# Weighted sums of gathered expert rows: on TensorE by accumulating transposes of rows that ScalarE has scaled, for more of the rows than before

## The chip, the cores and the metric

The kernel runs on one core of one Trainium2 chip. The metric is the device time of one execution in microseconds (us); the median of three runs of the kernel before is 3475.92 us, the lowest 3460.99 us, the highest 3478.14 us. A core has TensorE (PE, with its weight loads shown apart as PEld), VectorE (DVE), ScalarE (ACT), GpSimd (POOL), SyncE (SP), which starts most loads, and 16 DMA engines that all queues share.

## The reference

Three blocks of a network run one behind the other on 512 tokens of 1024 features in float32: a first block (two feed-forwards around a mixer of a gated recurrence and a 31-tap convolution), a second block (a mixer with a gated delta rule, then a layer of experts), and a third block (a mixer of retention and a state space, then a feed-forward). What the change touches is the layer of experts at the end of the second block:

```
ids, gates = peer_routing(h2, ...)          # per token 8 heads x 16 experts = 128 experts
# per token: a[s] = gelu(u[id_s] . h2) * gate_s     for s = 0..127
#            ff   = sum over s of a[s] * v[id_s]    v: rows of 1024 numbers
x = x + gt2 * ff
return rms_norm(x, final_norm_w)
```

So each token needs 128 rows of a table u and 128 rows of a table v, each of 4 KB, gathered by number. The 512 tokens need 512 gathers of u and 512 of v, a gather being one row for each of 128 tokens, 512 KB.

## The kernel before, in words

The tokens lie in four tiles of 128 (tokens on the partitions), and the tiles in two halves of two tiles. The halves run one behind the other: the experts of half 0 run beside the first two blocks of half 1, and those of half 1 beside the third block of half 0 (`experts`, line 1761). Ahead of that stretch lie the first two blocks of half 0, behind it the third block of half 1.

Each engine takes its instructions in the order in which the program wrote them. The program writes the other half's phases and puts steps of the experts in between: `tick` (line 130) adds to a credit at a pace that the table `ZONE` sets for each phase, and takes the next step of the experts from the list `self.fill` whenever the credit allows. A step is one gathered tile of u or v. In the steady part the steps alternate: u of head h+1, v of head h (`order`, line 1210). The names of the phases in `ZONE` are x and g (opening, products of the first mixer), h (gated recurrence), c (convolution), f (feed-forward of the first block), m (products of the second mixer), d (delta rule), R (routing, and products of the third mixer), r (retention), s (state space), F3 (feed-forward of the third block and what is left of the experts).

A step i first starts gathers (`fetch`, line 1162, from GpSimd's queue) until 8 beyond i are under way, then works on its own. The gathered tiles, and five long-lived ones (the two h2, the running sum `acc`, and two of `finish`), share 15 buffers named `gu`; a gather waits until a buffer is free. `u_step` (line 1168) is one VectorE instruction over 128x1024 that multiplies by h2 and sums along the row into one column of `act`; after 16 of them ScalarE applies gelu and VectorE the gate.

`v_step` (line 1177) adds a[s] times a v tile to the sum, on one of two engines. The second number of `ZONE` is the share that TensorE takes: it adds up in `vcredit`, and when this reaches 1 the step goes to TensorE. There ScalarE makes a diagonal matrix dg (128x128, the identity scaled by the column a[s], two buffers), and TensorE multiplies dg with the v tile, as two products of 512 columns that accumulate in two PSUM banks over the whole tile of tokens. Every other step is one VectorE instruction, acc = v * a[s] + acc, over 128x1024. Step 127 of a tile always goes to TensorE. `finish` (line 1196) adds the two sums, applies the modulation, adds to x and normalises.

Other names: `bcast_row` (line 696) spreads a column over rows by four transposes a bank and a copy by ScalarE; `psum` (line 163) takes one of 8 PSUM banks; `put_mix` (line 829) transposes with four instructions a call.

Of the kernel before, what the change touches and what calls it, by code (L numbers as in the profile page):

```python
# [11 lines left out]
F32 = mybir.dt.float32  # L12
# [9 lines left out]
NT = 4          # token tiles  # L22
NH = 2          # token tiles of a half: the halves run one behind the other
# [11 lines left out]
# Costs of steps, in the unit of tick and idle: a transfer of 512 KB, a step of the routing, the end of a token tile  # L35
DMA, ROUTE, FINISH = 1.46, 0.8, 6.0
AHEAD = 8           # gathers under way ahead of their use
GB = 15             # their buffers
# the hidden blocks of the feed-forwards that run piece by piece in the gaps of the other half
ASIDE1 = (4, 4, 4, 4, 4, 2)  # L40
ASIDE3 = (4,) * 4
FIRST3 = 16          # hidden blocks of the third feed-forward of half 0 beside the last experts
ADA = 28             # tiles of the modulation beside the first feed-forward, the others beside the second
CONV_PE = (0, 2)     # blocks of the long convolution on TensorE, by half
# by phase: pace of the steps of the experts, share of their sums that TensorE takes
ZONE = dict(x=(1, 0.5), g=(1, 0.35), h=(1.15, 0.41), c=(0.43, 0.4), f=(1.43, 0), m=(1.73, 0.06), d=(1.09, 0.4),
            R=(1.09, 0.39), r=(1.33, 0.3), F3=(1.1, 0), s=(1, 0.65))
# pieces let in by gap of TensorE
GAP = dict(_0=4, l=3, h=0.74, c=0.22, m=5.53, d=0.9, r=0.5, s=1.6, _4=5.2, ln=8, l4=8)
NORM = 4.82          # pace of a normalisation  # L50
WEIGHTS = 3          # of a tile of weights in float32
# rates of the steps: modulation beside the two feed-forwards, experts during the routing
RATE_ADA, RATE_ROUTE = (0.85, 0.6), (0.92, 2.17)
# the course of the phases beside the experts, the transfers of their own, and the share of the experts' steps to fit in
# [3 lines left out]
class Ker:  # L58
    def __init__(self, ctx, tc, I):
# [3 lines left out]
        self.exact = False      # products in float32 itself, not in parts  # L63
# [14 lines left out]
        self.aux = nc.gpsimd        # for what VectorE need not do, unless GpSimd has transfers to start  # L78
# [3 lines left out]
        # states: of the first and of the second block, then both of the third block's retention  # L82
# [13 lines left out]
    def xt(self, es, side=None):  # L96
        """transposed activations, split in two, for one phase"""
        xp = es.enter_context(self.tc.tile_pool(name="xt", bufs=1, side=side))
        self.XH, self.XL = self.pair(xp, "X", KD)

    def pair(self, pool, name, n, **k):
        """an operand of products, n blocks: in two parts, or whole"""
        if self.exact:
            return pool.tile([P, n, TH], F32, name=name + "H", **k), None
        return [pool.tile([P, n, TH], F32R, name=name + c, **k) for c in "HL"]
# [19 lines left out]
    def course(self, i):  # L125
        """the rate that spreads the steps of the experts over a phase"""
# [3 lines left out]
    def tick(self, d, load=0.0):  # L130
        """a phase goes on by d, with load for a transfer of its own: the steps of the other half's experts
        go in between so that the transfers are even"""
# [12 lines left out]
    def idle(self, d):  # L145
        """TensorE has little to do for d: pieces of the feed-forward set aside go in between"""
# [29 lines left out]
    def rsqrt(self, out, in_, scale, eps):  # L176
        """out = (in_ * scale + eps) ** -0.5: Newton's iteration from the halved exponent"""
# [43 lines left out]
    def ahead(self):  # L221
        """of the weights of a feed-forward set aside, split the next tile and load on"""
# [9 lines left out]
    def whole(gen):  # L232
        """all pieces of a generator at once; its value"""
# [12 lines left out]
    def g_fm(self, srcs):  # L246
        """feature-major blocks: out[f, i, t] = sum_k w_i[k, f] X[t, k]; srcs [128, 8*128]"""
# [16 lines left out]
    def g_tm(self, srcs, lhs, evac):  # L264
        """token-major: out[t, c] = sum_k lhs[k, t] w[k, c]; srcs: list of [128, 2, 512]; lhs(k) -> (H, L) [128, 512]"""
# [23 lines left out]
    def stats(self, y):  # L289
        """mean and variance over the free axis (1024 or 512)"""  # L290
# [12 lines left out]
    def g_transpose_x(self, src, scale=None, bias=None):  # L303
        """XH, XL <- split of (src^T * scale + bias); src(t, k) -> [128 t, 128 feat]"""
# [18 lines left out]
    def layer_norm(self, gname, bname, alpha):  # L323
        """x <- alpha * LN(x); XT <- split of LN(x)^T"""
# [35 lines left out]
    def g_ffn(self, parts, up, down, scale, fb=0):  # L360
        """x += scale * ffn; up(pool, j): generator of blocks j and j + 1 of the hidden layer, [128, 2, TH];
        down(k, c): weights of blocks k and k + 1"""
# [164 lines left out]
    def _hgrn(self, hp, uT, acc):  # L527
# [5 lines left out]
        # lower bound: softmax over the two rows, first row  # L533
# [128 lines left out]
    def ada_setup(self):  # L662
        """modulation vectors, feature-major: mod[:, 8*i + k] = feature 128*k + p of the i-th of six"""
# [24 lines left out]
    def wide(self, pool, name, key, n=D, at=0):  # L688
        """a row on all partitions; where transfers hold the time, from its columns on TensorE"""
# [6 lines left out]
    def bcast_row(self, out, colsv):  # L696
        """out[*, 128*k + p] = colsv[p, k]"""
# [18 lines left out]
    def g_rms_xt(self, xn, scale, bias):  # L716
        """xn[t] <- x * rstd; XT <- split of (xn^T * scale + bias)"""
# [29 lines left out]
    def softplus(self, pool, z, n):  # L747
        """z <- log(1 + exp(z)), accurate for any z"""
# [17 lines left out]
    def gemm_narrow(self, pool, src, n, meta=None):  # L766
        """token-major X @ w[:, :n] -> psum [128, (t, n)]; src [128, 8*n]; with the meta tokens from 256 on"""
# [22 lines left out]
    def _mixer2(self, mp):  # L790
# [5 lines left out]
        # q, k, v: short convolution and silu, feature-major  # L796
# [1157 lines left out]
```

## Time and profile before

| what | value |
|---|---|
| median of three runs | 3475.92 us (3460.99 to 3478.14) |
| span of the profiled execution, first to last instruction | 3464.7 us |
| the profiled execution's own time | not recorded apart from its span, which lies 3.7 us over the lowest run and 11.2 us under the median |
| PE, PEld busy share of the span | 87%, 68% |
| DVE, ACT, POOL busy share | 77%, 33%, 42% |
| mean granted TensorE clock | 0.932 of full speed |
| gathers' queue | 536.94 MB |
| all other loads | 417.29 MB |

The gathers begin at about 960 us and the last expert sum ends at about 2880 us. Busy shares are over the whole span; the rows further down give them by stretch. PE's ends are modelled, and a float32 product of 512 columns stands in the trace as two records, a transpose as one.

### The profile page before, as it was taken

The numbers are of one execution on the slowest core, as the hardware profiler recorded it, in microseconds if no ns is written. First come the engines' busy times: TensorE is split into PE (matmuls) and PEld (weight loads), VectorE is DVE, ScalarE is ACT, GpSimd is POOL, SyncE is SP. The second block draws the span as 40 slices with busy tenths as digits, with TensorE's granted clock in tenths as the row PEclk, the third lists the DMA queues.
The fourth block names the chain that finished last, engine by engine and source line by source line (L and its number), as shares of the span: only waits on it lengthen the run. The fifth ranks groups of instructions, "written<-read, shape, count | busy, mean of one in ns | idle before, by whom it ended". The sixth has DMA issues, their size and how long they took to land. (4 is left out here: it accounts for less than half of the span.)

```text
span 3464.7 us, 44842 instructions
## 1 busy us (share of the span) xinstructions
PE 3023.7 (87%) x15402; PEld 2350.9 (68%) x15402; DVE 2667.9 (77%) x6456; ACT 1145.3 (33%) x1687; POOL 1439.0 (42%) x1187
## 2 busy tenths in 40 slices
PE   9999999998979789987777867879797975999998
PEld 9987889888866357836354643536474745888897
DVE  7779686665588999878898999897877786566555
ACT  4454544553312242103222121112222213455554
POOL 0020000023245656655677567586767671211200
PEclk9999999999999899998899988899998987999999
DMA  8863477542389979998999899999999995644365
GB/s 312 279 194 118 131 267 233 168 161 86 105 303 357 355 263 384 409 402 325 381 326 375 335 339 391 347 368 357 333 365 359 396 409 193 182 133 139 119 188 162
DMA packets 276757, 957.10 MB, mean 276 GB/s; under 512 B 38304, under 2 KB 42144, under 8 KB 276528
## 3 DMA queue, kind: packets, MB, share of 16 engines
q0 software_dynamic: 147456, 536.94, 41.0%
q1 hardware_dynamic: 129072, 417.29, 35.6%
q8 instruction: 122, 2.00, 0.2%
q14 instruction: 107, 0.88, 0.1%
HBM read 947.81 MB, written 2.10 MB: 274 GB/s over the span
## 5 line engine op out<-in xcount | busy, mean ns | idle before, releaser
L1164 POOL DMA_INDIRECT gu<-in_peer_v,idx x512 | 633.6, 1238 | 317.1 <-issue 111.9
L1164 POOL DMA_INDIRECT gu<-in_peer_u,idx x512 | 609.3, 1190 | 349.6 <-issue 110.9
L1171 DVE SCALAR_TENSOR_TENSOR gu<-gu 128x1024 f32<-128x1024 f32 x512 | 620.7, 1218 | 59.4 <-DMA gu<-in_peer_u,idx 55.7
L203 DVE TENSOR_TENSOR wL<-wr,wH 128x1024 fp32r<-128x1024 f32 x332 | 409.1, 1234 | 249.2 <-ACT wH L202 231.9
L256 PE MATMUL ps<-XH,wr 128*128 128x256 f32 x2368 | 528.7, 383 | 0.2 <-issue 0.2
L256 PEld LDWEIGHTS ps<-XH,wr 128*128 128x128 f32 x2368 | 450.9, 192 | 73.2 <-issue 12.8
L202 ACT CAST wH<-wr 128x1024 fp32r<-128x1024 f32 x332 | 348.3, 1050 | 440.3 <-PE ps L281 217.4
L1194 DVE SCALAR_TENSOR_TENSOR gu<-gu,act 128x1024 f32<-128x1024 f32 x366 | 467.6, 1278 | 28.6 <-DMA gu<-in_peer_v,idx 23.4
L1188 PE MATMUL ps<-gu,dg 128*128 128x512 f32 x568 | 306.5, 664 | 101.8 <-DMA gu<-in_peer_v,idx 67.4
L1188 PEld LDWEIGHTS ps<-gu,dg 128*128 128x128 f32 x568 | 112.7, 212 | 206.9 <-issue 158.2
L278 PE MATMUL ps<-wr,XH 128*128 128x512 f32 x512 | 229.1, 601 | 0.0
L256 PE MATMUL ps<-XH,wH 128*128 128x256 f32 x1408 | 206.5, 289 | 16.3 <-ACT XH L116 10.0
L256 PE MATMUL ps<-XH,wL 128*128 128x256 f32 x1408 | 202.4, 287 | 1.5 <-DVE wL L203 1.2
L256 PE MATMUL ps<-XL,wH 128*128 128x256 f32 x1408 | 203.0, 288 | 0.2
L256 PEld LDWEIGHTS ps<-XH,wH 128*128 128x128 f32 x1408 | 186.6, 196 | 21.9 <-ACT XH L116 13.7
L256 PEld LDWEIGHTS ps<-XH,wL 128*128 128x128 f32 x1408 | 185.6, 196 | 2.9 <-DVE wL L203 2.7
L203 DVE TENSOR_TENSOR fL<-fr,fH 128x1024 fp32r<-128x1024 f32 x98 | 126.1, 1288 | 79.5 <-ACT fH L202 50.1
L256 PEld LDWEIGHTS ps<-XL,wH 128*128 128x128 f32 x1408 | 186.5, 197 | 0.6 <-DVE XL L118 0.6
L278 PEld LDWEIGHTS ps<-wr,XH 128*128 128x128 f32 x512 | 98.0, 193 | 122.7 <-issue 120.3
L202 ACT CAST fH<-fr 128x1024 fp32r<-128x1024 f32 x98 | 102.6, 1047 | 175.4 <-PE ps L256 58.7
L1186 ACT ACTIVATE dg<-ident,act 128x128 f32<-128x128 f32 x142 | 55.1, 400 | 312.3 <-PE ps L1188 246.5
L184 POOL TENSOR_TENSOR r<-rx,mhalf 128x1 f32<-128x1 f32 x18 | 11.9, 669 | 330.7 <-DVE rx L182 330.7
(618 smaller groups left out, 5462.4 us busy)
## 6 DMA issues: line engine op xcount, KB each, us to landing
wr<-in_wi_fm SPq DMA_DIRECT2D x112, 512.0 KB
wr<-in_wi_tm SPq DMA_DIRECT2D x96, 512.0 KB
wr<-in_wf SPq DMA_DIRECT2D x96, 512.0 KB
wr<-in_wo SPq DMA_DIRECT2D x64, 512.0 KB
wa<-in_wada SPq DMA_DIRECT2D x48, 512.0 KB
wr<-in_f2g SPq DMA_DIRECT2D x44, 512.0 KB
wr<-in_f2u SPq DMA_DIRECT2D x44, 512.0 KB
wr<-in_f2d SPq DMA_DIRECT2D x44, 512.0 KB
```

The source lines that it names most:

```text
L184: nc.gpsimd.tensor_tensor(out=out, in0=x, in1=self.mhalf[:p, :].to_broadcast(list(out.shape)), op=ALU.pow)
L202: self.nc.scalar.copy(H, raw)
L203: self.nc.vector.tensor_tensor(out=L, in0=raw, in1=H, op=ALU.subtract)
L256: nc.tensor.matmul(ps[:, i * TH:(i + 1) * TH], a[:, k * P:(k + 1) * P], b[:, k, :], start=n == 0, stop=n == KD * len(terms) - 1)
L278: nc.tensor.matmul(pss[t], lh[:, ts], wh, start=k == 0, stop=k == nk - 1)
L1164: nc.gpsimd.indirect_dma_start(out=g, out_offset=None, in_=I[src], in_offset=bass.IndirectOffsetOnAxis(ap=idx[:, s:s + 1], axis=0))
L1171: nc.vector.scalar_tensor_tensor(g, g, 1.0, h2, op0=ALU.mult, op1=ALU.mult, accum_out=st["act"][:, s:s + 1])
L1186: nc.scalar.activation(dg, self.ident, AF.Copy, scale=c)
L1188: nc.tensor.matmul(st["ps"][i], dg, g[:, i * 512:(i + 1) * 512], start="pe" not in st, stop=s == 127)
L1194: nc.vector.scalar_tensor_tensor(st["acc"], g, c, st["acc"], op0=ALU.mult, op1=ALU.add)
```

## The change

Of the sums over v, those for TensorE are done in another way. ScalarE multiplies the gathered v tile itself, in place, by the column a[s] (128x1024 instead of the 128x128 diagonal). TensorE then adds the scaled tile to the sum by eight transposes of 128x128, which accumulate in the same two PSUM banks, so that the banks hold the sum transposed. These eight are written into the program only at the tile's next v step (`add_up`), except for step 127, whose own follow at once. `finish` copies the two banks to SBUF by ScalarE, transposes them back by eight transposes into two new banks, and goes on as before; the buffer that it copies into is filled with the row of the final norm afterwards, not before.

The second number of most entries of `ZONE`, TensorE's share, is raised: by a little under twice for most. The paces, `COURSE` and everything else stay. The diff also drops the comments, which is left out here.

```diff
-ZONE = dict(x=(1, 0.5), g=(1, 0.35), h=(1.15, 0.41), c=(0.43, 0.4), f=(1.43, 0), m=(1.73, 0.06), d=(1.09, 0.4),
-            R=(1.09, 0.39), r=(1.33, 0.3), F3=(1.1, 0), s=(1, 0.65))
+ZONE = dict(x=(1, 0.9), g=(1, 0.65), h=(1.15, 0.75), c=(0.43, 0.75), f=(1.43, 0), m=(1.73, 0.2), d=(1.09, 0.75),
+            R=(1.09, 0.7), r=(1.33, 0.6), F3=(1.1, 0.1), s=(1, 1))
...
+        def add_up(last=False):
+
+            g, st["wait"] = st["wait"], None
+            for i in range(2):
+                for j in range(4):
+                    k = 4 * i + j
+                    nc.tensor.matmul(st["ps"][i][:, j * P:(j + 1) * P], g[:, k * P:(k + 1) * P], self.ident,
+                                     is_transpose=True, start="pe" not in st and j == 0, stop=last and j == 3)
+            st["pe"] = True
+
         def v_step(s, g):
...
             c = st["act"][:, s:s + 1]
             self.vcredit += self.vshare
+            if st.get("wait") is not None:
+                add_up()
             if (self.vcredit >= 1.0 and s) or s == 127:
                 self.vcredit -= 1.0
-                dg = pp.tile([P, P], F32, name="dg", bufs=2)
-                nc.scalar.activation(dg, self.ident, AF.Copy, scale=c)
-                for i in range(2):
-                    nc.tensor.matmul(st["ps"][i], dg, g[:, i * 512:(i + 1) * 512],
-                                     start="pe" not in st, stop=s == 127)
-                st["pe"] = True
+                nc.scalar.activation(g, g, AF.Copy, scale=c)
+                st["wait"] = g
+                if s == 127:
+                    add_up(True)
...
             fw = pp.tile([P, D], F32, name="gu", bufs=GB)
-            self.bcast_row(fw, self.fw2)
+            for i in range(2):
+                nc.scalar.copy(fw[:, i * 512:(i + 1) * 512], st["ps"][i])
             for i in range(2):
                 c = slice(i * 512, (i + 1) * 512)
-                nc.vector.tensor_tensor(out=acc[:, c], in0=st["ps"][i], in1=acc[:, c], op=ALU.add)
+                pt = self.psum()
+                for j in range(4):
+                    nc.tensor.transpose(pt[:, j * P:(j + 1) * P], fw[:, (4 * i + j) * P:(4 * i + j + 1) * P], self.ident)
+                nc.vector.tensor_tensor(out=acc[:, c], in0=pt, in1=acc[:, c], op=ALU.add)
                 nc.vector.tensor_tensor(out=acc[:, c], in0=acc[:, c], in1=g2[:, c], op=ALU.mult)
                 nc.vector.tensor_tensor(out=y[:, c], in0=y[:, c], in1=acc[:, c], op=ALU.add)
+            self.bcast_row(fw, self.fw2)
```

## Rows read from the trace of the kernel before

**Rows 1.** The page's engines: busy us, share of the span, instructions.
```profile
PE 3023.7 (87%) x15402; PEld 2350.9 (68%) x15402; DVE 2667.9 (77%) x6456; ACT 1145.3 (33%) x1687; POOL 1439.0 (42%) x1187
```
**Rows 2.** Busy time by stretch, whole expert stretch: PE, PEld, DVE, ACT, POOL, clock, DMA.
```profile
955.00:2890.00 1935.00, 1587.64 (x6132) 1051.49 (x6130) 1678.63 (x4972) 416.81 (x766) 1242.88 (x1024) 0.90 0.94 355
```
**Rows 3.** The same, six stretches: phases h, d, routing, r, r, s.
```profile
1140.00:1240.00 100.00, 70.83 (x272) 41.17 (x272) 93.49 (x261) 23.91 (x44) 66.37 (x59) 0.86 0.90 324
...
1700.00:1840.00 140.00, 101.39 (x537) 71.77 (x536) 130.57 (x258) 34.55 (x61) 101.19 (x85) 0.87 0.92 328
...
1880.00:2040.00 160.00, 115.04 (x465) 80.62 (x464) 150.31 (x656) 38.53 (x72) 95.18 (x82) 0.86 0.91 343
...
2120.00:2200.00 80.00, 50.31 (x158) 28.05 (x157) 70.98 (x271) 11.66 (x21) 52.16 (x47) 0.79 0.95 355
...
2280.00:2360.00 80.00, 55.62 (x177) 30.54 (x176) 73.38 (x248) 13.77 (x24) 63.98 (x53) 0.85 0.98 375
...
2440.00:2520.00 80.00, 60.71 (x195) 33.11 (x194) 70.39 (x159) 22.95 (x49) 60.63 (x50) 0.89 0.90 332
```
**Rows 4.** The same: the first feed-forward, then two stretches of products in R.
```profile
1280.00:1540.00 260.00, 247.50 (x939) 178.51 (x938) 220.41 (x725) 36.99 (x53) 158.96 (x129) 0.97 1.01 395
...
2040.00:2120.00 80.00, 79.42 (x289) 46.25 (x288) 71.44 (x256) 15.66 (x30) 56.60 (x47) 1.00 1.01 377
...
2360.00:2440.00 80.00, 80.00 (x387) 58.05 (x386) 60.49 (x146) 20.56 (x42) 51.59 (x41) 0.98 0.96 356
```
**Rows 5.** Stretches, line 1188 alone: PE, PEld, clock, DMA; first and last of six.
```profile
1140.00:1240.00 100.00, 32.40 (x62) 11.52 (x62) 0.86 0.90 324
...
2440.00:2520.00 80.00, 28.77 (x57) 11.31 (x58) 0.89 0.90 332
```
**Rows 6.** Groups by line: engine, operation, count; busy us, mean ns; idle before.
```profile
L1194 DVE SCALAR_TENSOR_TENSOR gu<-gu,act 128x1024 f32<-128x1024 f32 x366 | 467.6, 1278 | 28.6 <-DMA gu<-in_peer_v,idx 23.4 <-issue 2.0 <-DVE rt L1303 0.7
L1188 PE MATMUL ps<-gu,dg 128*128 128x512 f32 x568 | 306.5, 664 | 101.8 <-DMA gu<-in_peer_v,idx 67.4 <-ACT dg L1186 23.6 <-issue 10.1
L1186 ACT ACTIVATE dg<-ident,act 128x128 f32<-128x128 f32 x142 | 55.1, 400 | 312.3 <-PE ps L1188 246.5 <-issue 37.7 <-DVE act L1175 14.7
L722 ACT ACTIVATE xn<-xres,r 128x1024 f32<-128x1024 f32 x12 | 13.3, 1141 | 11.0 <-DVE r L188 4.3 <-DVE rt L191 3.0 <-DVE r L192 2.8
```
**Rows 7.** Timeline of PE: start us, us, line, count of equal instructions.
```profile
1905.18 1.88 PE L1188 MATMUL ps<-gu,dg 128*128 128x512 f32 x4
...
1039.98 1.07 PE L702 MATMUL ps<-ident,grc 128*128 128x128 f32 x8 [2.13 <-DVE rt L1235]
1040.87 1.88 PE L702 MATMUL ps<-ident,brc 128*128 128x128 f32 x8
1042.55 2.78 PE L310 MATMUL ps<-ident,xres 128*128 128x128 f32 x16
```
**Rows 8.** Busy time by stretch around those transposes; the clock stands third from last.
```profile
1037.50:1040.80 3.30, 1.17 (x9) 0.85 (x9) 3.30 (x18) 0.52 (x2) 0.71 (x1) 1.00 0.30 37
1040.90:1044.30 3.40, 3.40 (x19) 3.40 (x18) 3.40 (x17) 2.68 (x6) 2.79 (x3) 0.50 0.87 310
1044.40:1047.00 2.60, 1.41 (x14) 1.21 (x13) 2.60 (x10) 2.60 (x7) 2.05 (x2) 1.00 0.89 265
```
**Rows 9.** Waits in 955 to 2890: us in total, times, longest us.
```profile
ACT dg L1186 <- PE ps L1188: 246.5, 75, 13.0
...
PE ps L1188 <- DMA gu<-in_peer_v,idx: 67.4, 12, 16.1
...
DVE gu L1171 <- DMA gu<-in_peer_u,idx: 55.7, 46, 16.5
...
POOL gu L1164 <- PE ps L1188: 31.6, 21, 4.4
```
**Rows 10.** Timeline at the end of the last tile's sums.
```profile
2863.87 15.79 DVE L1194 SCALAR_TENSOR_TENSOR gu<-gu,act 128x1024 f32<-128x1024 f32 x12
2872.79 3.75 PE L1188 MATMUL ps<-gu,dg 128*128 128x512 f32 x4 [16.12 <-DMA gu<-in_peer_v,idx]
```

## The prediction

> **What bounds the kernel now.** I read the page's engines first [rows 1]: PE 87%, DVE 77%. That is an average over three parts. The experts' gathers lie between 955 and 2890 us, so all that the change touches is in 1935 of 3464.7 us [rows 2]; ahead of it and behind it nothing is edited. In that part DVE is busy 1678.63 us (87%), the DMA engines 0.94 of the time, PE 1587.64 us, ACT only 416.81 us (22%). Three resources are close to full, so I went to single stretches. Two kinds show. In six stretches, where small products, evictions and vector work follow one another (gated recurrence, delta rule, routing, retention, state space), DVE is at 88 to 94% and PE at 63 to 76% with a clock of 0.79 to 0.89 [rows 3]. They are 640 us long together, DVE is busy 589.1 us of them (92%), DMA is at 0.92 on average (weighted by length). There VectorE is what the stretch waits for. In the stretches of large products PE is busy 79.42 and 80.00 of 80 us at clock 0.98 to 1.00, and DVE has room [rows 4]; TensorE sets their length. In the feed-forward of the first block DMA stands at 1.01 and 395 GB/s [rows 4]: I take 1.01 for what "full" looks like here. The waits agree: VectorE waits for landings of u only 55.7 us in 46 places [rows 9], so rows mostly lie ready before VectorE gets to them.
>
> **How many sums move.** Working the credits of `tick` through the program's order gives where the 512 v steps fall: x 4, g 13, h 36, c 3, f 73, m 48, d 45, R 163, r 26, s 41, F3 60. Times the shares this is 141.4 before and 261.4 after; with the forced step 127 of each tile and the carry of `vcredit` it is 142 and 262. The trace has 142 diagonals on ScalarE and 568 records of products [rows 6], four for each step. So 120 sums leave VectorE: R 52, d 15, h 13, s 13, m 9, r 7, F3 6, g 4, x 1.
>
> **VectorE.** 120 x 1278 ns [rows 6] = 153 us less.
>
> **TensorE.** Four records of a step take 1.88 us, the last one's own length is 0.59 us at full clock, so they start 0.43 us apart: a step holds TensorE 4 x 0.43 = 1.72 us [rows 7]. A transpose is one record. Eight took 1.07 us with a last one of 0.28 us, so (1.07 - 0.28) / 7 = 0.11 us apart [rows 7]: a step of eight holds it 0.9 us. Before 142 x 1.72 = 244 us, after 262 x 0.9 = 236 us: TensorE's work stays about the same though it has nearly twice the sums. No row shows a transpose that accumulates. From below it costs 0.11 us as these do; from above, were it worked as a float32 product, two records of 0.11, 0.22 us, and 461 us in all. I take 0.11: adding in PSUM costs the products nothing either, as they start as regularly.
>
> A row that bears on the clock: at 1040.9 us the granted clock fell to 0.50 (1.2 GHz), after a stretch in which PE was busy 1.17 of 3.30 us, and in the 3.40 us that followed PE ran transposes alone; behind them the clock was 1.00 again [rows 8], and the eight that began there took 1.88 us, the eight ahead of them 1.07 us [rows 7]. The Trainium skill, page "TensorE: Matmul & The Clock Gate", section "Part 4: PE-mode transpose", says that transposes do not count as activity for the clock gate, so that the full clock isn't granted for them, and that one took about 275 ns in a kernel. By its figure the sums would hold TensorE an estimated 262 x 8 x 0.275 = 576 us, 332 us more than now. Here the trace disagrees: the clock rose on transposes alone. I keep the rule as a rival.
>
> **ScalarE.** A diagonal costs 0.40 us, and the same form as the new instruction, 128x1024 with a scale by column, 1.141 us [rows 6]. 142 x 0.40 = 57 us become 262 x 1.141 = 299 us: +242 us, which takes ScalarE from 22% to 34% of the part. It lies beside other work unless a phase's eviction stands right behind it in ScalarE's queue. The new instruction waits for the gather's landing, which the diagonal did not; queued behind it are copies out of PSUM that TensorE and VectorE wait for. On the other hand ScalarE no longer waits for TensorE to release one of two diagonals, 246.5 us in 75 places now, and TensorE no longer waits for a landing itself (67.4 us in 12 places [rows 9]): it comes to the eight transposes one v step later. What is late next is VectorE's u step, at the same place in the order. Bounds: nothing gained from the waits, to 134 us of added ScalarE time in the six stretches (below) all in the chain. I take 4 us lost, near the low end, as ScalarE is busy only 15 to 29% there [rows 3].
>
> **Buffers.** A tile on TensorE is now held for one v step more. GpSimd's gathers waited for those products 31.6 us in 21 places [rows 9]; with 262 / 142 as many it would be 58 us, +27. Bounds 0 and 27; I take 2, since a gather that starts late costs only where the rows aren't ready in advance.
>
> **finish.** Each of the four adds two copies by ScalarE (0.6 us, half of a 1.14 us one), eight transposes (0.9 us) and hand-overs, some 3 us. At the end of the last tile VectorE ends its twelve sums at 2863.87 + 15.79 = 2879.66 us, TensorE its own at 2876.54 [rows 10]: 3.1 us of cover for the new steps, and the other three have gathers running ahead. I take 0; without cover 4 x 3 = 12 us.
>
> **The sum.** In the six stretches TensorE has 62, 67, 72, 26, 32 and 57 records (the first and last in [rows 5]), 316 / 4 = 79 steps; at 262 / 142 it will be 146, 67 more. VectorE loses 67 x 1.278 = 86 us of 589 and would be at 79%. These stretches could shrink by as much, but their bytes must still come: at 0.92 of the time now, against 1.01 when full, DMA leaves 640 x (1 - 0.92 / 1.01) = 57 us. So 0 to 57 us; I take 38, two thirds of it, because VectorE is the fuller one but the round trips from engine to engine remain. In four stretches of products in R (two of them in [rows 4]; 139 records) 35 x 1.72 = 60 us of TensorE become 64 x 0.9 = 58: 2 us. The other 120 - 67 - 29 = 24 sums, 31 us of VectorE, lie in the opening, m and F3, mostly beside full DMA: 0 to 31, I take 8. Together 38 + 2 + 8 - 4 - 2 = 42 us. The profiled span of 3464.7 us would become 3423; what lies around it stays, and as that span is 11.2 us under the median of the runs, the median becomes 3475.9 - 42 = 3434 us.
>
> **Rivals.**
> *All of it turns into time.* VectorE is the only bound of the six stretches and DMA gets fuller than 1.01 of any stretch: 57 + 2 + 31 = 90 us, 3386 us. For it: 92% busy. Against it: 395 GB/s in the fullest stretch, 324 to 375 in the six [rows 3, 4].
> *Hidden anyway.* The six stretches are held by the chain through TensorE, and by DMA at 0.94 on average [rows 2], so that a lighter VectorE only waits more: within 17 us, some 3470 us. For it: three resources near full. Against it: few waits of VectorE for landings.
> *ScalarE's queue, slower.* In the six stretches ScalarE gets 146 x 1.141 - 79 x 0.40 = 135 us more. Where a scaling stands right before a copy that TensorE waits for, its 1.14 us is added to the round trip, while VectorE's 1.28 us leaves it. It decides once more than 86 of the 135 us, 64%, lie in that chain; with all of them it is 135 - 86 = 49 us slower, 3525 us. For it: PE, ACT and DVE take turns in these phases, and ScalarE now stops at landings. Against it: ScalarE is idle over 70% of the time.
> *The clock, slower.* If transposes don't hold the clock, it stays at 0.50 in the six stretches, whose mean is 0.86 and in which PE is busy 453.9 us: 453.9 x 0.86 / 0.50 = 781 us in 640, 141 us slower, 3617 us. Against it: [rows 8]. That is what the page's rule would do here.
>
> **How the numbers follow.** Forecast (18 to 75 us gained) 0.50, all of it (over 75) 0.14, hidden 0.20, ScalarE's queue 0.12, clock 0.04. 0.5%, 17 us, is what a measurement of this kernel can tell; so faster 0.64, same 0.20, slower 0.16. The likeliest case alone spans 3401 to 3458. The range for 8 in 10 goes down to 3382, just past the case in which all turns into time, and up to 3486, which takes in the hidden case and a third of the price of ScalarE's queue.
>
> **What would show it.** 262 scalings of 128x1024 on ScalarE at about 1.14 us; 2096 transposes 0.11 us apart at full clock; 250 sums left on VectorE; VectorE near 80% and DMA up to 0.97 or more in phases h, d, routing and s; stretches of products unchanged in length; the part from the first gather to the last sum some 40 us shorter. Wrong would be: transposes 0.2 us apart, a lower granted clock than 0.90 over the part, long waits of TensorE for ScalarE's scaling, or GpSimd waiting for transposes far over 58 us.

## The result and the profile after

The changed kernel takes 3490.86 us (median of 5 runs), the kernel before beside it 3465.52 us: a ratio of 1.0063, 95% interval 1.0044 to 1.0082, so 22 us slower. I had forecast 3434 us, 42 us faster, from the median of the first three runs, 3475.92 us; that of the five beside the changed kernel is 10 us lower. A second measurement beside other kernels gave 1.0043 (1.0030 to 1.0056). The times differ a little from one chip to the next, so below only ratios are compared, each to runs of the kernel before on the same chip.

What the change does came out as counted. The engines of the page after, then its groups by line (columns as in [rows 6], which they answer to; the scaling is L1197, the transposes L1183, VectorE's v sums L1204):

```profile
PE 3030.0 (87%) x16962; PEld 2508.2 (72%) x16962; DVE 2541.6 (73%) x6336; ACT 1366.5 (39%) x1806; POOL 1406.1 (40%) x1187
```
```profile
L1204 DVE SCALAR_TENSOR_TENSOR gu<-gu,act 128x1024 f32<-128x1024 f32 x246 | 315.1, 1281 | 48.1 <-DMA gu<-in_peer_v,idx 43.6 <-issue 2.9
L1183 PE MATMUL ps<-ident,gu 128*128 128x128 f32 x2096 | 315.0, 300 | 143.0 <-ACT gu L1197 136.9 <-issue 5.9
L1197 ACT ACTIVATE gu<-gu,act 128x1024 f32<-128x1024 f32 x262 | 296.0, 1147 | 399.2 <-DMA gu<-in_peer_v,idx 332.5 <-DVE gu L1204 12.2 <-issue 11.3
```

262 scalings at 1.147 us, 2096 transposes, 246 sums left on VectorE (366 before; four more are the plain products that open each tile). VectorE's v sums take 315.1 us in place of 467.6, as counted; by the engines' row VectorE is busy 126 us less than in [rows 1] and TensorE 6 us more. And yet the time grew. The waits of the same part as in [rows 9] (us in total, times, longest us):

```profile
ACT gu L1197 <- DMA gu<-in_peer_v,idx: 332.5, 73, 40.3
...
PE ps L1183 <- ACT gu L1197: 136.9, 40, 22.9
DVE gu L1171 <- DMA gu<-in_peer_u,idx: 85.8, 86, 3.0
...
POOL gu L1164 <- PE ps L1183: 37.9, 18, 24.0
...
POOL gu L1164 <- ACT gu L1197: 27.8, 23, 7.4
```

ScalarE used to wait for TensorE to give back a diagonal; now it waits for landings, in 73 places. TensorE's waits for landings (67.4 us) have become waits for the scaling behind the landing, and grew to 136.9: one of the signs of being wrong that the prediction had named. ScalarE's idle time ahead of these instructions grew less, from 312.3 us ahead of diagonals [rows 6] to 399.2.

Where the time went I read by pairing equal products: the n-th TensorE instruction of a line (the sums left out) is the same work in both traces, and the difference of its start is how late the kernel is there. Before against after: 2 us late at 1010, 14 at 1090, 36 at 1321, where the feed-forward of phase f begins, 28 in phase d, 37 in the routing, 17 at 2352, 26 at the end. So nearly all is lost between 1040 and 1321 us, in x, g, h and c, where the prediction had put a gain in sum, and phase d, one of the heaviest in sums, gives nothing back.

Phases h, d, routing, r, r and s of [rows 3], bounded by the same products in the trace after (columns: stretch, length, busy us of PE, PEld, DVE, ACT, POOL, clock, DMA share, GB/s):

```profile
955.00:2920.00 1965.00, 1597.04 (x7689) 1210.59 (x7688) 1547.59 (x4855) 637.90 (x887) 1210.05 (x1026) 0.89 0.93 349
1152.00:1265.00 113.00, 71.79 (x423) 57.57 (x423) 96.41 (x395) 42.62 (x53) 66.51 (x61) 0.83 0.80 277
1722.00:1868.00 146.00, 104.95 (x734) 96.51 (x734) 115.45 (x244) 62.40 (x81) 96.17 (x84) 0.85 0.90 316
1906.00:2074.00 168.00, 119.98 (x655) 106.30 (x654) 137.48 (x621) 66.50 (x89) 96.44 (x85) 0.83 0.91 345
2154.00:2227.00 73.00, 51.75 (x233) 37.64 (x231) 68.17 (x337) 24.68 (x29) 53.38 (x44) 0.79 0.96 357
2307.00:2377.00 70.00, 55.44 (x258) 38.12 (x257) 50.66 (x108) 24.66 (x28) 48.85 (x45) 0.88 1.02 399
2460.00:2545.00 85.00, 62.94 (x329) 47.55 (x328) 65.30 (x155) 42.16 (x59) 59.76 (x51) 0.78 0.91 328
```

VectorE fell from 93 to 79% in d and from 94 to 82% in the routing, as forecast, but those stretches are 146 us against 140 and 168 against 160. DMA did not rise there (0.90 and 0.91; 0.97 or more was the sign). Only the two of phase r are shorter (73 and 70 against 80), and in the second DMA is full (1.02).

The place with TensorE's largest single wait in the opening, in phase h: ScalarE's timeline after, then TensorE's (start us, us, line, count, idle before and what ended it).

```profile
1139.23 1.15 ACT L1197 ACTIVATE gu<-gu,act 128x1024 f32<-128x1024 f32 x1 [2.64 <-DVE acc L500]
1140.28 1.05 ACT L584 COPY qT<-ps 128x512 f32<-128x512 f32 x2
1155.73 1.15 ACT L1197 ACTIVATE gu<-gu,act 128x1024 f32<-128x1024 f32 x1 [14.39 <-DMA gu<-in_peer_v,idx]
1161.04 1.15 ACT L1197 ACTIVATE gu<-gu,act 128x1024 f32<-128x1024 f32 x1 [4.16 <-DMA gu<-in_peer_v,idx]
1162.10 0.56 ACT L563 COPY vv<-ps 128x512 f32<-128x512 f32 x1
...
1168.75 0.23 ACT L1309 ACTIVATE gate<-gate 128x32 f32<-128x32 f32 x1 [4.79 <-DVE gate L1308]
...
1169.35 0.59 ACT L598 COPY kT<-ps 128x512 f32<-128x512 f32 x1
```
```profile
1147.18 1.04 PE L1183 MATMUL ps<-ident,gu 128*128 128x128 f32 x8
1148.06 0.60 PE L596 MATMUL ps<-ident,kk 128*128 128x128 f32 x4
1148.49 1.04 PE L1183 MATMUL ps<-ident,gu 128*128 128x128 f32 x8
1170.00 2.08 PE L604 MATMUL ps<-qT,kT 128*128 128x128 f32 x8 [20.47 <-ACT kT L598]
```

kT's copy out of PSUM needs the four transposes of L596, done by 1149. It runs 20 us later. Some 13 of these are two scalings ahead of it in ScalarE's queue that wait for their rows; most of the other 7 are a gate of the routing, also ahead of it, that waits for VectorE. Before, this copy was late too, by 12 us, behind an activation of 16 results of u steps:

```profile
1121.11 1.28 ACT L1174 ACT_TABLE_LOAD   x1
1146.19 0.22 ACT L1174 ACTIVATE act<-act 128x16 f32<-128x16 f32 x1 [23.80 <-DVE gu L1171]
1146.31 0.39 ACT L1186 ACTIVATE dg<-ident,act 128x128 f32<-128x128 f32 x1
1146.60 1.05 ACT L563 COPY vv<-ps 128x512 f32<-128x512 f32 x2
1147.55 0.60 ACT L598 COPY kT<-ps 128x512 f32<-128x512 f32 x1
```

One correction to what stands ahead of the prediction: the order on an engine is not that of the program's text. The framework that builds the kernel sorts each engine's instructions. With fewer v sums on VectorE it put other work there earlier: in the list of VectorE's instructions 361 of the routing and 63 sums of the short convolution stand ahead of phase h's second token tile, against 298 and 14 before, and the traces show the same shift. So each change of a share also changes the order, here and in every experiment.

### The profile page after: what moved, and what is told of

It is laid out like the page before. It is cut to its first block, busy times and chain, and to the rows that moved or that the text cites. A ratio compares the mean times of both kernels' runs of the same rounds, so it can differ in the third digit from the quotient of the medians.

```text
span 3490.5 us, 47918 instructions
## 1 busy us (share of the span) xinstructions
PE 3030.0 (87%) x16962; PEld 2508.2 (72%) x16962; DVE 2541.6 (73%) x6336; ACT 1366.5 (39%) x1806; POOL 1406.1 (40%) x1187
## 4 chain that ended last, share of the span: by engine, by line
PE 27%; DVE 9%; DMA 7%; issue 3%; ACT 2%; POOL 2%; another core or an unknown queue 0%; SPq 0%; DVEq 0%; ACTq 0%; POOLq 0%
PE ps L256 9%; DMA gu<-in_peer_v,idx 4%; DVE gu L1171 3%; PE ps L278 3%; PE ps L1183 3%; DMA gu<-in_peer_u,idx 3%; PE ps L280 2%; PE ps L281 2%; PE ps L282 2%; POOL gu L1164 1%; PE ps L1399 1%; DVE rt L1318 1%; ACT gu L1197 1%; DVE gu L1204 1%; PE ps L785 1%
## 5 line engine op out<-in xcount | busy, mean ns | idle before, releaser
L1164 POOL DMA_INDIRECT gu<-in_peer_u,idx x512 | 618.5, 1208 | 375.3 <-issue 123.5
L1164 POOL DMA_INDIRECT gu<-in_peer_v,idx x512 | 590.4, 1153 | 355.2 <-issue 130.4
L256 PE MATMUL ps<-XH,wr 128*128 128x256 f32 x2368 | 536.7, 386 | 0.0
L1197 ACT ACTIVATE gu<-gu,act 128x1024 f32<-128x1024 f32 x262 | 296.0, 1147 | 399.2 <-DMA gu<-in_peer_v,idx 332.5
L1183 PE MATMUL ps<-ident,gu 128*128 128x128 f32 x2096 | 315.0, 300 | 143.0 <-ACT gu L1197 136.9
L1183 PEld LDWEIGHTS ps<-ident,gu 128*128 128x128 f32 x2096 | 274.0, 157 | 200.0 <-ACT gu L1197 156.7
L1204 DVE SCALAR_TENSOR_TENSOR gu<-gu,act 128x1024 f32<-128x1024 f32 x246 | 315.1, 1281 | 48.1 <-DMA gu<-in_peer_v,idx 43.6
```

The source lines that it names most:

```text
L256: nc.tensor.matmul(ps[:, i * TH:(i + 1) * TH], a[:, k * P:(k + 1) * P], b[:, k, :], start=n == 0, stop=n == KD * len(terms) - 1)
L1164: nc.gpsimd.indirect_dma_start(out=g, out_offset=None, in_=I[src], in_offset=bass.IndirectOffsetOnAxis(ap=idx[:, s:s + 1], axis=0))
L1183: nc.tensor.matmul(st["ps"][i][:, j * P:(j + 1) * P], g[:, k * P:(k + 1) * P], self.ident, is_transpose=True, start="pe" not in st and j = ...
L1197: nc.scalar.activation(g, g, AF.Copy, scale=c)
L1204: nc.vector.scalar_tensor_tensor(st["acc"], g, c, st["acc"], op0=ALU.mult, op1=ALU.add)
```

## The experiments

The theories: 1, ScalarE's queue: scalings wait for landings with copies that TensorE needs behind them (1a: in phases x and g, ahead of phase h's first copies). 2, the larger shares themselves, by whatever method. 3 and 6, tiles held longer, so that gathers start late. 4, VectorE's order. 5, the clock. All ratios are to the kernel before.

**e1_method.** The table `ZONE` of before in the changed kernel, so the method alone.

> The new way of taking a sum (scaling on ScalarE, eight accumulating transposes), with the shares of before: 142 scalings, no sum more on TensorE. Theory 1 (ScalarE's queue: the scaling waits for a gather's landing, and copies out of PSUM that TensorE needs stand behind it; in the changed kernel ScalarE waits 332.5 us for landings in 73 places, and 36 us are lost between 1040 and 1321 us): with 142 / 262 of the scalings and nothing taken from VectorE a loss against before of 10 to 25 us, lost between 1040 and 1321 us again. Rival 2 (the shares: more sums on TensorE in the opening phases are what loses, however they are done): the time of before within 8 us. Rival 3 (buffers: a tile is held for one v step more, gathers start late): a loss of 10 to 25 us too, but with GpSimd waiting for transposes or scalings and not ScalarE for landings ahead of the copies that come late.

1.0056 (1.0042 to 1.0070): the method alone costs 19 us with 142 sums. That is theory 1's size. Of its place a part shows: TensorE's products start 8 us late at the beginning of f, and the rest is lost here and there behind it. Nearly all of these 8 us arise near 1045 us, where the first mixer's products begin. ScalarE and TensorE in e1, then in c_before:

```profile
1048.69 1.15 ACT L1197 ACTIVATE gu<-gu,act 128x1024 f32<-128x1024 f32 x1 [6.70 <-DMA gu<-in_peer_v,idx]
1049.75 3.73 ACT L316 ACTIVATE XH<-ps,bf,gf 128x256 f32<-128x256 f32 x8
...
1050.35 16.67 PE L278 MATMUL ps<-wr,XH 128*128 128x512 f32 x32 [4.62 <-ACT XH L316]
```
```profile
1044.78 3.76 ACT L316 ACTIVATE XH<-ps,bf,gf 128x256 f32<-128x256 f32 x8 [0.27 <-PE ps L310]
...
1046.78 13.90 PE L278 MATMUL ps<-wr,XH 128*128 128x512 f32 x32
```

In e1 ScalarE stops 6.70 us at a scaling whose rows haven't landed, and behind it stand the activations that the first products need. TensorE waits 4.62 us for them; in the 4.7 us after that its granted clock is 0.50, where c_before has 1.00, and the 32 products take 16.67 us, not 13.90. By the pairing against c_before, 7 to 9 us are lost between 1042 and 1056 us in nine of the eleven kernels here that scale on ScalarE and give TensorE sums of x and g, and 2 and 3 us in the other two (e8, q1). In all others, e4 among them, which scales on VectorE, it is under 2 us. So theory 1 holds at this place; how much of it is left at the end isn't shown.

The sum of ScalarE's stops, on the other hand, explains nothing: it stands idle 275.8 us ahead of scalings in e1, less than the 312.3 ahead of diagonals before.

**e2_shares.** The new table in the kernel before.

> The old way (diagonals on ScalarE, four records of products for a step) with the new shares: some 262 sums on TensorE at 1.72 us, 451 us against 244. Theory 1 (ScalarE's queue): the opening between 1040 and 1321 us loses less than the 36 us of the changed kernel, as a diagonal of 0.40 us waits for no landing; behind it TensorE's 207 us more cost in the stretches of products (64 - 35 steps x 1.72 = 50 us) against up to 38 us from VectorE: 3465 to 3500 us in all. Rival 2 (shares): the opening loses about the same 36 us, and the whole is above 3500 us.

1.0135 (1.0118 to 1.0151), 3499.32 us against 3451.66. TensorE is busy 160 us more, so the whole says little; but f begins 29 us late against the first profile of the kernel before (36 in the changed kernel), without a single scaling. That speaks for theory 2, and against 1 as the only cause.

**e3_late**, and **e9_method_late** with the old table:
```
+ if st.get("pend") is not None:          # the v step before
+     pg, pc = st["pend"]
+     nc.scalar.activation(pg, pg, AF.Copy, scale=pc)
+     st["wait"], st["pend"] = pg, None
...
- nc.scalar.activation(g, g, AF.Copy, scale=c); st["wait"] = g
+ st["pend"] = (g, c)
...                                      # step 127: scaled and added up at once
```


> The changed kernel, with each scaling written one v step later (and its transposes one v step behind that): when ScalarE comes to it the rows should mostly have landed, as VectorE has passed another step or two. A tile is held for one v step more. Theory 1 (ScalarE's queue): ScalarE's wait for landings falls from 332.5 us to under 150, the opening gets back at least 20 of its 36 us, the whole is 3450 to 3472 us. Rival 2 (shares): 3485 to 3495 us, as the changed kernel. Rival 3 (buffers): 3495 us or more, with GpSimd waiting longer than the 66 us for transposes and scalings of the changed kernel.

> The new method with the shares of before, each scaling written one v step later. Theory 1 (ScalarE's stops at landings cost the method its 19 us): a ratio of 1.002 or less, ScalarE's wait for landings down from 203.8 us to under 120. Theory 5 (the clock): 1.0045 to 1.0065, as without the shift.

e3 1.0040 (1.0027 to 1.0053), e9 1.0056 (1.0042 to 1.0069). ScalarE still waits 289.4 + 47.3 us for landings in e3 and 167.1 + 76.0 in e9 (203.8 in e1). One step later is not late enough to take the wait away, so theory 1 is not really tested by it; the expected 20 us of the opening did not come back.

**e4_vector.** `nc.vector.tensor_scalar(g, g, c, None, op0=ALU.mult)` in place of the scaling on ScalarE.

> The changed kernel with the scaling done by VectorE (a 128x1024 tensor_scalar is 0.745 us there) in place of ScalarE: 262 x 0.745 = 195 us go to VectorE, which against before then has 195 - 153 = 42 us more. Shares and transposes as changed. Theory 1 (ScalarE's queue): ScalarE waits for no landing of v, the opening gets back most of its 36 us, and the whole is 3455 to 3485 us, within 15 us of before. Rival 2 (shares) and rival 3 (buffers): the opening loses its 36 us as before, and VectorE's work comes on top: 3500 us or more.

1.0086 (1.0073 to 1.0099). TensorE's wait for kT went from 20.5 to 0.2 us, and the opening was late all the same: TensorE now waited 25.7 us for VectorE's E (L627) in one place. Taking ScalarE out of the chain moves the wait to another engine; VectorE, busy 155 us more than in the changed kernel, is no free place for it.

**c_before and c_after**, the two kernels once more, for profiles on one chip.

> The kernel before, unchanged, for a profile on the same chip as the others of this set. Each theory: a ratio of 1.000 within 0.001. With it, where the other kernels lose is read against a run of the same chip; in the first profile of it the part from 1005 to 1350 us is what I compare.

> The changed kernel, unchanged, for a profile on the same chip. Each theory: a ratio of 1.006 within 0.002; the products of the first block's feed-forward (from some 1350 us on) come 25 to 40 us later than in the kernel before of the same chip.

1.0004 (0.9994 to 1.0015) and 1.0043 (1.0030 to 1.0056). Here f begins 17 us late, and the profiled execution of the changed kernel was the fastest of its five (3455.39, the others 3464 to 3467). So one profile's delay may be off by 10 us and more; the ratios decide. The six stretches together, bounded by the same products: 632 us before, 624 after, a gain of 8, not 38; d and the routing 140 and 160 before, 140 and 162 after.

**e6_open_old and e7_late_open_old.** `x=(1, 0.5), g=(1, 0.35), h=(1.15, 0.41), c=(0.43, 0.4)` in the changed kernel; e7 with the scaling one v step later too.

> The changed kernel with the shares of before in the opening phases alone (x, g, h, c: some 18 sums fewer on TensorE), the new shares everywhere behind. Theory 4, which the last set suggests (with a lighter VectorE the 60 sums of the second half's short convolution are issued ahead of the last of phase h's vector steps; in the kernels with the new shares all 60 stand ahead of them, with the old shares 18, and the opening lost 34 to 40 us in the first and 11 in the second; here 18 again): the opening loses no more than 15 us, and the whole gains at least 15 us on the changed kernel, a ratio to before of 0.997 to 1.002. Theory 1 (ScalarE's queue alone): 18 of 262 scalings go, so at most a tenth of the loss: 1.005 or more.

> Both edits together: the shares of before in the opening, and each scaling written one v step later. If theory 4 holds for the opening and theory 1 (ScalarE's stops at landings) for what lies behind it, the two add up: 25 us from the opening on top of the 8 us that the late scaling was worth, a ratio of 0.993 to 0.999. If the late scaling was worth nothing, as the run before it.

1.0013 (1.0001 to 1.0025) and 0.9997 (0.9986 to 1.0008): 19 sums fewer on TensorE (265 on VectorE against 246) take away 10 us of the 15 lost (6 either way); f begins 5 and 9 us late. The rest of the table (101 more sums on TensorE behind the opening, 265 on VectorE against 366) is worth 15 us, again 6 either way: 1.0056 of e1 against 1.0013.

**p2_after_pinned and p3_before_pinned.** VectorE's order held in the second half (edges of order only; the conditions are left out here):
```
+ with self.tc.issue_after(self.last_h): self._conv31(cvp, uT, acc)   # behind phase h
+ with self.tc.issue_after(self.last_u): f()                          # each routing step
```


> The changed kernel, with the order of VectorE's instructions in the second half's opening held to that of the program: the short convolution's sums go behind phase h's last vector step, each routing step behind the u step that stands ahead of it. In the list of VectorE's instructions 249 routing instructions and no convolution sum then stand ahead of phase h's second token tile, against 361 and 63 in the changed kernel and 298 and 14 in the kernel before. Theory 4 (where sums leave VectorE, other work is issued ahead there, and phase h comes later): the opening gets back at least 15 us, ratio 0.995 to 1.001. Rival 2 (it is TensorE's larger share itself that costs in the opening, whatever the order): 1.003 to 1.008.

> The kernel before with the same order held: 253 routing instructions and no convolution sum ahead of phase h's second token tile, against 298 and 14. A control: theory 4 gives it little, as little stood out of order: 0.996 to 1.002. If it gains as much as the changed kernel does, the order is a matter of its own, apart from the change.

1.0076 (1.0063 to 1.0089) and 1.0019 (1.0009 to 1.0028). Theory 4 falls: with the program's order held the changed kernel is no faster. Nor is order nothing: by itself it cost the kernel before 7 us (p3) and the changed kernel some 11 (p2 against c_after). The same 40 us of c_before and of p2 (columns as above):

```profile
1140.00:1180.00 40.00, 29.57 (x117) 17.69 (x118) 40.00 (x118) 10.68 (x21) 27.19 (x25) 0.87 0.94 336
```
```profile
1140.00:1180.00 40.00, 13.92 (x74) 10.09 (x73) 10.63 (x23) 12.04 (x16) 13.60 (x12) 0.70 0.56 176
```

VectorE is idle for 29 of 40 us and f begins 26 us late all the same. So in p2 it isn't VectorE's work that makes the opening late: between 1120 and 1180 VectorE itself waits for rows (23.6 us in 7 places), GpSimd for the buffers that VectorE's u steps give back (19.1 us in 5), ScalarE for rows (40.3 us in 5), TensorE for ScalarE's kT (23.3 us). That the other work on VectorE only filled such a hole in the changed kernel too is likely, but not shown: there VectorE is busy 35 of these 40 us.

**e8_twice.** The old table, each transpose issued twice and `scale=0.5` on the copy out of PSUM.

> The new method with the shares of before (142 sums), each accumulating transpose run twice and the total halved when it is copied out of PSUM: 142 x 0.87 = 124 us more of TensorE, about what the products with diagonals held it. The new method alone had a ratio of 1.0056 and a granted clock of 0.83 between 2300 and 2880 us, where the kernel before has 0.90. Theory 5 (TensorE, less busy, is granted less clock, and the products and transposes of these phases take longer): the clock comes back to 0.88 or more there, the ratio is 1.003 or less. Rival (the clock doesn't matter, ScalarE's queue does): 1.0056 or more.

1.0070 (1.0056 to 1.0084). The stretch from 2300 to 2880 us, first of e1, then of e8:

```profile
2300.00:2880.00 580.00, 412.02 (x1925) 303.73 (x1926) 463.12 (x986) 153.04 (x235) 402.92 (x327) 0.83 0.96 360
```
```profile
2300.00:2880.00 580.00, 456.29 (x2381) 351.50 (x2379) 464.12 (x982) 157.25 (x238) 399.71 (x327) 0.87 0.96 362
```

The clock rose from 0.83 to 0.87 (0.912 to 0.930 over the whole run), 0.88 was expected, and the time did not fall. Theory 5 finds no support; a gain from the clock could only hide behind the 97 us that TensorE is busy more (3019.8 against 2923.1). Both together, 1136 transposes more and the higher clock, cost some 5 us (1.0070 against 1.0056, and the intervals overlap), so most of TensorE's own time for the sums looks like slack.

**q1_buffer.** `GB = 16`; `rv` 6 for 8 buffers and `mrep` 1 for 2 to make room.

> The changed kernel with 16 buffers for gathered tiles in place of 15 (room for it from two fewer small tiles of the routing and one of its scratch tiles). Theory 6 (tiles held for TensorE leave too few buffers, GpSimd's gathers start one at a time and DMA falls to 0.62 to 0.67 between 1130 and 1180 us, where the old shares have 0.95): DMA there 0.8 or more, the copy of kT less than 15 us late, ratio 1.002 or less. Theory 1a (v steps queued on ScalarE and TensorE ahead of phase h's first copies): the copy of kT still some 20 us late, ratio 1.004 to 1.006.

1.0079 (1.0064 to 1.0094), DMA at 0.57 between 1130 and 1180, kT 21.4 us late. One buffer more does not help, so theory 6 finds no support; the smaller pools of the routing may have cost something of their own.

**q2_xg_vector and q3_xg_new.** `x=(1, 0), g=(1, 0)` with the new h and c; `h=(1.15, 0.41), c=(0.43, 0.4)` with the new x and g.

> The changed kernel with no sum of phases x and g on TensorE (x=0, g=0; in the changed kernel 0.9 and 0.65, some 12 of 17 steps), the new shares in h, c and behind. Theory 1a (v steps of x and g queued ahead of phase h's first copies): TensorE's wait for kT 13 us or less (19.5 and 20.5 in two profiles of the changed kernel), DMA 0.9 or more between 1130 and 1180 us, the opening within 10 us of the kernel before, ratio 1.002 or less. Rival (the shares of h and c are what costs): wait for kT about the same as before the change but the opening 15 us or more late, ratio 1.0035 or more.

> The other half: the new shares in x and g, the old ones in h and c, the new ones behind. Theory 1a: TensorE's wait for kT some 20 us, DMA about 0.6 between 1130 and 1180 us, ratio 1.0035 or more. Rival (h and c): ratio 1.002 or less.

1.0012 (1.0001 to 1.0023) and 1.0005 (0.9996 to 1.0015). Either half put back (12 and 13 sums) recovers most of the loss, so neither expectation holds alone. In the profiles f begins 9 us late in q2 and 24 in q3, which makes up 17 behind it. And kT is no good mark: TensorE waits 18.7 us for it in q2, 22.2 in q3.

**q4_best and r2_drs.** q4 as e7 with `x=(1, 0), g=(1, 0)`; r2 also with the old m, R and F3.

> What helped, together: scaling written one v step later, no sum of x and g on TensorE, the old shares in h and c, the new shares from phase m on. If theory 1a holds it is a little better than the 0.9997 of the late scaling with the old opening: 0.995 to 0.999, faster than both kernels. If the opening was only the question of how many sums TensorE takes in all: 0.9985 to 1.0015.

> The new method with the scaling one v step later; the new shares in d, r and s alone, the old ones in h, c, m, R and F3, none of x and g on TensorE. In the routing stretch of R TensorE waited 35.7 us for scalings with the new shares, against 25.4 us for diagonals and landings in the kernel before. If the new shares pay only in the stretches that VectorE sets: 0.996 to 0.999, faster than both kernels. If the sums of R pay as well: 0.9995 to 1.002.

0.9991 (0.9980 to 1.0002) and 1.0006 (0.9994 to 1.0018). q4 beats the changed kernel; whether it beats the kernel before can't be told. Nor is r2 faster than both, as it should be if the new shares paid only in the stretches that VectorE sets; whether the sums of R pay can't be told, as the intervals of q4 and r2 overlap.

**r1_before_xg.** The kernel before, its own method, with `x=(1, 0.9), g=(1, 0.65)` alone: VectorE's sums go from 366 to 360, so 6 more on TensorE (I had expected 5).

> The kernel before, its own method, with the new shares in phases x and g alone (0.9 and 0.65): 5 sums more on TensorE in the whole kernel, 6 us less for VectorE, nothing else. Theory 1a (what stands on TensorE and ScalarE ahead of phase h's first copies sets the opening, whatever the method): TensorE's wait for kT 17 us or more (11.8 in the kernel before), the opening 10 us or more late, ratio 1.002 or more. Rival (5 sums are too few; it takes the new method): within 5 us, 0.9985 to 1.0015.

1.0055 (1.0041 to 1.0069): 6 sums of 512, 8 us of VectorE's work, cost 19 us. f begins 14 us late. Theory 1a's mark fails again (kT 5.1 us); the loss itself came from the two opening phases' shares, the only edit. But that edit reaches further than six sums: x and g add 4 x 0.4 + 13 x 0.3 = 5.5 steps of credit, so the carry of `vcredit` moves by half a step and other sums behind them go to TensorE too. Behind the first 74 u steps the number of v sums that VectorE does between two u steps differs in 227 of 439 places (in 6 between the two profiles of the kernel before). And q3, with the same shares in x and g but the new method, lost 2 us, not 19. So no run shows that the sums of x and g by themselves cost 19 us. TensorE's waits between 1005 and 1360 us in r1, and below it in c_before:

```profile
PE ps L631 <- DVE E L627: 12.1, 5, 10.8
PE ps L835 <- DVE osq L1047: 11.7, 1, 11.7
PE ps L310 <- DVE xres L345: 11.0, 2, 9.9
...
PE ps L604 <- ACT kT L598: 5.8, 2, 5.1
```
```profile
PE ps L604 <- ACT kT L598: 11.8, 1, 11.8
PE ps L835 <- DVE osq L1047: 8.4, 1, 8.4
PE ps L310 <- DVE xres L345: 6.2, 1, 6.2
PE ps L631 <- DVE E L627: 3.8, 4, 2.5
```

One wait went, three grew. Over all 20 profiles, each against c_before, the beginning of f sorts by the shares of x and g: 14 to 51 us late in the nine with the new ones (either method, any order), -3 to 10 us in ten of the eleven others (e8, 19 us, is the exception). The lateness of f is not the loss, though: q3 is 24 us late there and loses 2 in all, e1 8 us and 19.

## Why the prediction was wrong

**Prices and counts: right.** 262 sums, 1.147 us against 1.141, and eight transposes in 1.04 us: with 0.27 for the last one still 0.11 us apart, as [rows 7] had it, also where they accumulate. VectorE's v sums fell by 152 us, 153 forecast; its busy time in all fell by 126. The granted clock over the part was 0.89 after 0.90: a hundredth under the sign that the prediction had named, but nowhere near the 0.50 of the clock's rival, which fell. The Trainium skill, page "TensorE: Matmul & The Clock Gate", section "Part 4: PE-mode transpose", gives some 275 ns for a transpose in a kernel. As the length of one the trace agrees, 273 ns in the median of the 2096. But the next one starts after 0.11 us, so the prediction's estimate of 576 us, which took the length for the time that each holds TensorE, was a misreading.

**"I take 38" for the six stretches: the step that failed by most.** The prediction said that VectorE is what these stretches wait for, since it is busy 92% of them. VectorE fell to 79 to 82% in d and routing as said, and these stretches kept their length (146 after 140 and 168 after 160 us in the first pair of profiles, 140 after 140 and 162 after 160 in the second). So the bound, 57 us and two thirds of it, was the error: a high busy share was read as a wait. p2 shows the same in 40 us of phase h, with VectorE idle for 29. Only the two stretches of r shrank, and in one of them DMA filled up to 1.02; the six together gained 8 us in the second pair. The new shares behind the opening are worth 15 us (e6 against e1), about a third of the 48 (38 + 2 + 8) that I had for the whole; the whole table is worth 5 (c_after against e1, within the noise).

**"ScalarE ... I take 4 us lost": mis-sized too.** The method alone cost 19 us (e1), where I had 4 for ScalarE, 2 for buffers and 0 for `finish`. I had bounded ScalarE's term by its added busy time in the six stretches, and chose the low end since ScalarE is idle there. Idle was the wrong measure: of its 399 us of idle time ahead of scalings, 332.5 are spent stopped at one of them with everything behind it stopped too, and what counts is whether TensorE needs what stands behind. Near 1045 us it does, and 7 to 9 us are lost there. That such stops are the rest of the method's price is not shown: e9 didn't remove them, e4, which took them off ScalarE, put work on VectorE instead, and before the change ScalarE stood idle 312 us ahead of diagonals, mostly for TensorE, without that price.

**"The other 24 sums ... 0 to 31, I take 8": no gain shown.** The opening was in this term, and its lower bound was zero since VectorE could only get lighter. But the opening's shares cost the changed kernel 10 us (c_after against e6), and those of x and g cost the kernel before 19 us (r1), with what they shift behind them. My reading is that there a chain of small steps of the other half goes round all engines, and that a v step on TensorE puts its place into the queues of two engines, not one; no run isolates that.

Put together: +19 for the method, -15 behind the opening, +10 in it, 14 us. These are differences along one row of kernels (before, e1, e6, c_after), so that they meet c_after's 15 us is no test of them. The first measurement, 22 us, is some way above.

**The rivals.** Of those I had, "ScalarE's queue, slower" comes nearest, with its mechanism in part and its place wrong: it was to happen in the six stretches at 49 us. "Hidden anyway" describes d and the routing. TensorE at 236 us against 244 and the buffers' waits (65.7 us against my 58) were near what I had said; that neither matters is supported by e8 (97 us more of TensorE's busy time, some 5 us) and q1 (a buffer more, no gain). No run isolates `finish`.

**Still open.** Which wait of the opening decides: kT in the changed kernel, E in e4, E, osq and xres in r1. It moves with each kernel, since a share changes the order of everything behind it. Then why the method costs 19 us with the shares of before, apart from the 7 to 9 us near 1045. And a rival to all these parts stands untested: order alone moved the two kernels by 7 and 11 us (p3, p2), every edit here changes the order, and no run repeats one edit under several orders. So some of the 19, 15 and 10 us may be luck of the order.

## What to carry to other kernels

A busy share of 92% does not say that the stretch waits for that engine: look for what the engine itself waits for, and ask whether the stretch would end earlier if its work were gone. When work moves from one engine to two others, count the instructions that will stand behind it in their queues and what data it will stop for; idle time there is no cover if the queue is in order. And never give a term a lower bound of zero because one engine gets less to do: try the smallest part of the change by itself, as r1 did with 6 sums of 120, and beside it an edit of the order alone, as p3 was, to know what order by itself is worth.

## What the runs showed of the hardware that I had not expected

Transposes that accumulate in PSUM run at the pace of plain ones, 0.11 us apart at full clock. The granted clock rose with TensorE's busy time (0.83 to 0.87 in e8, busy 412 and 456 of 580 us), and the time did not fall. Two profiles of the changed kernel, on two chips, differ by 25 us in how late f begins and by 37 us in their spans (3490.5 and 3453.6; of the kernel before 3464.7 and 3451.4), so a single profile of a kernel whose phases pass waits on from one to the next places a loss only roughly.
